# Attention scores with a zero-padded rotated key: every score matmul on 128 rows

## The chip, the cores and the metric

The kernel runs on one core of one Trainium2 chip, as one program. The metric is device time in microseconds (us). TensorE does the matmuls (in the profile PE, and PEld for its weight loads), VectorE is DVE, ScalarE is ACT, GpSimd is POOL, and SyncE (SP) issues most of the transfers.

## The reference, cut to what matters

The model is a trunk of four layers on 256 tokens of width 1024, all in float32. Layer 1 mixes tokens by multi-head latent attention with 8 heads. A query or key of a head has 128 plain values and 64 rotated ones, and the rotated key is the same for all heads:

```
q_rope = apply_rope(q_rope, cos, sin)
k_rope = apply_rope(k_rope[:, :, None, :], cos, sin)
k_rope = jnp.broadcast_to(k_rope, (B, S, MLA_HEADS, MLA_ROPE))
q = jnp.concatenate([q_nope, q_rope], axis=-1)
k = jnp.concatenate([k_nope, k_rope], axis=-1)
...
s = jnp.einsum('bqhd,bkhd->bhqk', qi, k).astype(jnp.float32) * scale
s = jnp.where(kpos[None, :] <= qpos[:, None], s, -jnp.inf)
p = jax.nn.softmax(s, axis=-1).astype(v.dtype)
```

A score is therefore a sum over 128 + 64 products.

## The kernel before, in words

Activations lie with their features on the 128 partitions and the 256 tokens along the free dimension. Projections are done in three matmuls each (`mm3`, L237 to L240): the weights and the activations are split into a high and a low part of type fp32r, and high times high, high times low and low times high are added up. Weights come by DMA in pieces of 1 MB (`raw`), and ScalarE casts the high part (`wh`, L207), VectorE subtracts for the low part (`wl`, L208). A Tile scheduler puts the instructions of every engine into an order at build time, and each engine then works through its own list, waiting on semaphores.

Layer 1 is the function `mla`. The tile `qr` has 8 slices of 256 columns: slices 0 to 3 hold the rotated queries, two heads to a slice (an even head in partitions 0 to 63, an odd one in 64 to 127), slice 4 the rotated key `kr`, which stands in both halves of the partitions alike, slices 5 and 6 the cosines `cs` and sines `sn`, and slice 7 the causal `mask`. `rope` makes a rotated slice in three VectorE steps (L733 reads the cosines, L734 the sines, L735 adds). The plain queries and keys are `qn` and `kn`; the keys are copied out of PSUM by ScalarE, two heads at a time (L765).

The loop behind `es = []` runs over heads. In turn h it issues, in this order, the scores of head h, in turn 1 the values (`vv`, L771, and ScalarE's copies L772), the transposes of head h - 2 (`turn`, L809), and the weighing of head h - 3 (`weigh`, L818 to L820). From head 2 on the transposes follow the scores at once. Between them stand steps of the output projection (`wo`) and of the conditioning vectors (`adaps`, L293, matmuls with 32 output columns).

`scores(h)` makes four matmuls into one PSUM tile `sc`: for the first 128 queries against 128 keys, and for the second 128 against 256 keys, each time a plain one on 128 rows (L788) and a rotated one on 64 rows (L789), which adds to it. They are plain float32, not fp32r; the trace has two records for each of them ("x2"). Behind them VectorE adds the mask (L791), takes the maximum (L792) and scales it (L793), ScalarE takes the exponential (L795), VectorE inverts the sum (L796), and the two share the normalization (L799, L801). Its result `e` is what `turn` transposes; ScalarE copies that to `pts` (L811).

Of the kernel before, what the change touches and what calls it, by code (L numbers as in the profile page):

```python
# [20 lines left out]
P = 128  # L21
# [70 lines left out]
def build(ctx, tc, A, out, stages=None):  # L92
    nc = tc.nc
    pe, act, dve, pool = nc.tensor, nc.scalar, nc.vector, nc.gpsimd
# [8 lines left out]
    def big(name, shape=(P, 2048), dt=F32):  # L103
        return tp.tile(list(shape), dt, tag="big", name=name, bufs=10)
# [4 lines left out]
    def t2(name, shape=(P, 512), dt=F32):  # L109
        return tp.tile(list(shape), dt, tag="t2", name=name, bufs=3)  # L110

    def sm(name, w, dt=F32):
        return tp.tile([P, w], dt, tag="sm", name=name, bufs=6)
# [4 lines left out]
    def misc(name, shape=(P, 512)):  # L118
        return pp.tile(list(shape), F32, tag="misc", name=name, bufs=3)
# [353 lines left out]
    def hilo(name, n):  # L473

        t = [[], []]
        for i in range((n + 7) // 8):
            for e in range(2):
                t[e].append(big(f"{name}{'hl'[e]}{i}", (P, 8, S), F32R))

        def view(e):  # L480
            def at_(c, w=1):
                v = t[e][c // 8]
                return v[:, c % 8, :] if w == 1 else v[:, c % 8 : c % 8 + w, :]

            return at_

        return view(0), view(1)
# [209 lines left out]
    def mla(l):  # L697
# [3 lines left out]
        qr = tables.pop()  # L701
        kr, cs, sn = (qr[:, i, :] for i in (4, 5, 6))
# [64 lines left out]
        def values(b, w=w):  # L767
            for t in range(2):
# [2 lines left out]
                mm3(ps[:], ch[:, 2, t * P : t * P + P], cl[:, 2, t * P : t * P + P], a, bl, True, True)  # L771
                act.copy(vv[:, t, 512 * b : 512 * b + 512], ps[:])  # L772

        yh, yl = hilo("o", 8)
        mask = qr[:, 7, :]
        pool.memset(mask, 0.0)
# [1 line left out]
        spans = ((0, P), (P, S))  # L778

        def scores(h):  # L780
            r0 = 64 * (h % 2)
            s = misc("sc")
            e = t2("e", (P, 384))
            mx = sm("mx", 2)
            nb = sm("nb", 2)
            su = sm("su", 2)
            for t, (o, n) in enumerate(spans):
                pe.matmul(s[:, o : o + n], qn[:, h, t * P : t * P + P], kn[:, h, :n], start=True, stop=False)  # L788
                pe.matmul(s[:, o : o + n], qr[r0 : r0 + 64, h // 2, t * P : t * P + P], kr[r0 : r0 + 64, :n], start=False, stop=True)  # L789
            for t, (o, n) in enumerate(spans):  # L790
                dve.tensor_tensor(e[:, o : o + n], s[:, o : o + n], mask[:, S - n : S], op=ALU.add)  # L791
                dve.tensor_reduce(mx[:, t : t + 1], e[:, o : o + n], axis=AX.X, op=ALU.max)  # L792
            dve.tensor_scalar_mul(nb[:], mx[:], -scale)  # L793
            for t, (o, n) in enumerate(spans):
                act.activation(e[:, o : o + n], e[:, o : o + n], AF.Exp, bias=nb[:, t : t + 1], scale=scale, accum_out=su[:, t : t + 1])  # L795
            dve.reciprocal(su[:], su[:])  # L796
            for t, (o, n) in enumerate(spans):
                if ESACT >> t & 1:
                    act.activation(e[:, o : o + n], e[:, o : o + n], AF.Copy, scale=su[:, t : t + 1])  # L799
                else:  # L800
                    dve.tensor_scalar_mul(e[:, o : o + n], e[:, o : o + n], su[:, t : t + 1])  # L801
            return e
# [22 lines left out]
        for h in range(8 + LAG + OLAG):  # L825
            if h < 8:
                es.append(scores(h))
            for b in range(2):
                if h == VVAT[b]:
                    values(b)  # L830
            if LAG <= h < 8 + LAG:
                turn(h - LAG, es[h - LAG])
            i = h - LAG - OLAG
            if i >= 0:
                weigh(i)
                if i % 2:
                    wo.step(i // 2)
            if h < MLA_ADA:
                ada_run("p")
# [324 lines left out]
    for kind, l in stages:  # L1164
# [3 lines left out]
        if kind == "mix":  # L1168
# [33 lines left out]
            elif l == 1:  # L1202
                modulated(l, 0)
                mla(l)
            else:
                modulated(l, 0)
                hgrn(l)
# [102 lines left out]
```

## Time and profile before

| | |
|---|---|
| time, median of 3 runs | 1388.17 us (1386.49 to 1388.37) |
| the profiled execution: its time, and its span from first to last instruction | 1391.3 us, 1389.6 us |
| PE busy in the span | 1358.8 us (98%) |
| DVE busy | 1091.6 us (79%) |
| ACT busy | 770.8 us (55%) |
| POOL busy | 17.2 us (1%) |
| granted TensorE clock, mean | 0.995 |

Times in the rows of the trace are from the start of the span. A busy share counts overlapping matmuls once, so a PE at 98% can still lose time between its matmuls: how far apart two matmuls start says more than how long each record is.

### The profile page before, as it was taken

How to read it: one execution, taken by the hardware profiler on the slowest of the kernel's cores; microseconds unless marked ns; L12 is line 12 of the kernel's file. 1: busy time of each engine (PE TensorE's matmuls, PEld its weight loads, DVE VectorE, ACT ScalarE, POOL GpSimd, SP SyncE). 2: the span in 40 equal slices, each digit the busy share in tenths (PEclk: the TensorE clock that was granted, in tenths of full speed). 3: DMA queues.
4: the chain of work that ended last, by engine and by line, in shares of the span. 5: the costliest groups of instructions: out<-in, count | busy, mean ns of one | idle time of the engine just before them, and what ended most of it. 6: DMA issues, size and time to landing. Idle time of an engine off the chain costs nothing.

```text
span 1389.6 us, 29284 instructions
## 1 busy us (share of the span) xinstructions
PE 1358.8 (98%) x12372; PEld 1286.1 (93%) x12372; DVE 1091.6 (79%) x1760; ACT 770.8 (55%) x1201; POOL 17.2 (1%) x17
## 2 busy tenths in 40 slices
PE   8999999999999999999989999999999999999997
PEld 6799999999987899999987889999987999999997
DVE  5699698889786698897788879889764964888853
ACT  3764366664465566654655646665456653666633
POOL 0100000000000000000010000000001000000000
PEclk9999999999999999999999999999999999999999
DMA  9869955468775276589475577558737465455531
GB/s 383 330 249 337 379 189 214 178 215 346 324 273 213 98 263 245 211 331 372 173 271 194 235 281 296 194 208 322 254 125 258 178 217 182 151 184 182 183 122 31
DMA packets 49483, 326.23 MB, mean 235 GB/s; under 512 B 5956, under 2 KB 9028, under 8 KB 11974
## 3 DMA queue, kind: packets, MB, share of 16 engines
q1 hardware_dynamic: 47568, 322.72, 61.9%
q8 instruction: 97, 1.59, 0.5%
q10 hardware_dynamic: 1784, 1.65, 0.4%
q14 instruction: 34, 0.28, 0.1%
HBM read 323.29 MB, written 1.05 MB: 233 GB/s over the span
## 4 chain that ended last, share of the span: by engine, by line
PE 92%; DVE 3%; DMA 3%; ACT 2%; issue 1%; DVEq 0%; SPq 0%; ACTq 0%
PE up L239 12%; PE up L238 12%; PE up L240 12%; PE dn L238 4%; PE dn L239 4%; PE dn L240 4%; PE go L238 2%; PE go L239 2%; PE go L240 2%; PE u L239 2%; PE u L238 2%; PE u L240 2%; PE adaps L293 2%; PE v L238 2%; PE v L239 2%; PE v L240 2%
## 5 line engine op out<-in xcount | busy, mean ns | idle before, releaser
L207 ACT CAST wh<-raw 128x1024 fp32r<-128x1024 f32 x426 | 434.9, 1031 | 395.5 <-PE up L239 171.4
L208 DVE TENSOR_TENSOR wl<-raw,wh 128x1024 fp32r<-128x1024 f32 x426 | 511.7, 1206 | 162.9 <-ACT wh L207 160.9
L238 PE MATMUL up<-hh,wh 128*128 128x256 f32 x1408 | 398.4, 284 | 2.6 <-ACT hh L444 2.5
L240 PE MATMUL up<-hh,wl 128*128 128x256 f32 x1408 | 398.3, 283 | 0.0
L239 PE MATMUL up<-hlo,wh 128*128 128x256 f32 x1408 | 398.2, 284 | 0.1
L238 PEld LDWEIGHTS up<-hh,wh 128*128 128x128 f32 x1408 | 270.5, 192 | 5.3 <-ACT hh L444 4.5
L239 PEld LDWEIGHTS up<-hlo,wh 128*128 128x128 f32 x1408 | 270.4, 192 | 0.6 <-DVE hlo L445 0.5
L240 PEld LDWEIGHTS up<-hh,wl 128*128 128x128 f32 x1408 | 270.8, 193 | 0.0
L238 PE MATMUL dn<-gh,wh 128*128 128x256 f32 x528 | 149.9, 284 | 1.5 <-ACT y L1089 1.5
L239 PE MATMUL dn<-gl,wh 128*128 128x256 f32 x528 | 149.4, 283 | 0.0
L240 PE MATMUL dn<-gh,wl 128*128 128x256 f32 x528 | 149.4, 283 | 0.0
L315 DVE CUSTOM_DVE_ANT_0 adaw<-adaw,cbc,prm 128x1024 f32<-128x1024 f32 x104 | 131.3, 1276 | 2.2 <-DMA adaw<-adad 2.2
L1089 ACT ACTIVATE y<-up,cwb 128x256 f32<-128x256 f32 x176 | 98.6, 560 | 10.1 <-DVE y L1091 9.8
L238 PEld LDWEIGHTS dn<-gh,wh 128*128 128x128 f32 x528 | 101.3, 192 | 2.0 <-ACT y L1089 1.7
L239 PEld LDWEIGHTS dn<-gl,wh 128*128 128x128 f32 x528 | 101.3, 192 | 0.0
L240 PEld LDWEIGHTS dn<-gh,wl 128*128 128x128 f32 x528 | 101.3, 192 | 0.0
L1091 DVE SCALAR_TENSOR_TENSOR y<-up,cwb,y 128x254 f32<-128x254 f32 x176 | 84.5, 480 | 4.7
L1090 DVE SCALAR_TENSOR_TENSOR y<-up,cwb,y 128x255 f32<-128x255 f32 x176 | 83.9, 477 | 0.8 <-ACT y L1089 0.8
L238 PE MATMUL u<-hh,wh 128*128 128x256 f32 x256 | 73.9, 289 | 0.0
L238 PE MATMUL go<-yh,wh 128*128 128x256 f32 x256 | 73.3, 287 | 0.0
L240 PE MATMUL u<-hh,wl 128*128 128x256 f32 x256 | 72.4, 283 | 0.0
L239 PE MATMUL u<-hlo,wh 128*128 128x256 f32 x256 | 72.4, 283 | 0.0
(337 smaller groups left out, 2478.8 us busy)
## 6 DMA issues: line engine op xcount, KB each, us to landing
raw<-up SPq DMA_DIRECT2D x88, 1024.0 KB, 4.8
adaw<-adad SPq DMA_DIRECT2D x52, 1024.0 KB, 8.1
adaw<-adap SPq DMA_DIRECT2D x36, 1024.0 KB, 7.5
raw<-dn SPq DMA_DIRECT2D x32, 1024.0 KB, 4.8
raw<-gmu SPq DMA_DIRECT2D x16, 1024.0 KB, 4.8
raw<-gmo SPq DMA_DIRECT2D x16, 1024.0 KB, 4.8
raw<-gmv SPq DMA_DIRECT2D x15, 1024.0 KB, 6.3
raw<-dn SPq DMA_DIRECT2D x16, 768.0 KB, 5.5
```

Of the source, the lines that this page charges most:

```text
L207: act.copy(wh[:, :w], raw[:, o : o + w])
L208: i = dve.tensor_tensor(wl[:, :w], raw[:, o : o + w], wh[:, :w].bitcast(F32), op=ALU.subtract)
L238: pe.matmul(ps, lh, rh, start=start, stop=False)
L239: pe.matmul(ps, lh, rl, start=False, stop=False)
L240: i = pe.matmul(ps, ll, rh, start=False, stop=stop)
L293: pe.matmul(ps[32 * j : 32 * j + 32, :], crep(kc), raw[:, k, j, :], start=kc == 0, stop=kc == KC - 1, tile_position=(0, 32 * j))
L315: dve.tensor_tensor_reduce(raw[:, e, :], raw[:, e, :], cbc[:], 1.0, prm[:, c0 : c0 + 1], ALU.mult, ALU.add, mod[:, l, b : b + 1])
L1089: act.activation(y[:], ps[:, e, :], AF.Identity, bias=b, scale=w[2])
L1090: dve.scalar_tensor_tensor(y[:, 1:], ps[:, e, : S - 1], w[1], y[:, 1:], op0=ALU.mult, op1=ALU.add)
L1091: dve.scalar_tensor_tensor(y[:, 2:], ps[:, e, : S - 2], w[0], y[:, 2:], op0=ALU.mult, op1=ALU.add)
```

## The change

Slice 5 of `qr`, whose cosines are not read after the last rotated query, becomes a second key `kro`. ScalarE copies the lower half of the key (partitions 64 to 127) there; GpSimd then writes zeros into that half of `kr`, and into partitions 0 to 63 of `kro`. So `kr` holds the key for even heads over zeros, and `kro` zeros over the key for odd heads. The rotated matmul now takes all 128 partitions of the query slice, which holds both heads of a pair, and the zeros take the other head's products out of the sum. The scores are the same.

```
+        kro = qr[:, 5, :]
+        act.copy(kro[64:P, :], kr[64:P, :])
+        pool.memset(kr[64:P, :], 0.0)
+        pool.memset(kro[0:64, :], 0.0)
+        krs_ = (kr, kro)
...
         def scores(h):
-            r0 = 64 * (h % 2)
             s = misc("sc")
...
                 pe.matmul(s[:, o : o + n], qn[:, h, t * P : t * P + P], kn[:, h, :n], start=True, stop=False)
-                pe.matmul(s[:, o : o + n], qr[r0 : r0 + 64, h // 2, t * P : t * P + P], kr[r0 : r0 + 64, :n], start=False, stop=True)
+                pe.matmul(s[:, o : o + n], qr[:, h // 2, t * P : t * P + P], krs_[h % 2][:, :n], start=False, stop=True)
```

Every engine keeps its order otherwise; three instructions are added, and lines behind them move down by 5. On ScalarE this is the place just before the first scores, with the semaphores that each waits for; `kn` are the plain keys, `wh` casts of later weights. Before:

```order
L207 CAST wh_1024_4912<-raw_4822 128x1024 [waits PE_49,Activation_49]
L207 CAST wh_0_5137<-raw_4906 128x1024 [waits DMAHW2_49,DVE_49,PE_49]
L765 COPY kn<-kn 128x512 [waits PE_49] x3
L207 CAST wh_1024_5141<-raw_4906 128x1024 [waits DVE_49,PE_49]
L765 COPY kn<-kn 128x512 [waits PE_49]
L772 COPY vv<-vv 128x512 [waits DMAHW1_49,PE_49,Pool_49]
```

And with the change:

```order
L207 CAST wh_0_5140<-raw_4906 128x1024 [waits DMAHW2_49,DVE_49,PE_49]
L765 COPY kn<-kn 128x512 [waits PE_49]
L776 COPY qr<-qr 64x256 [waits DVE_49]
L765 COPY kn<-kn 128x512 [waits PE_49] x2
L207 CAST wh_1024_5144<-raw_4906 128x1024 [waits PE_49,Activation_49]
L765 COPY kn<-kn 128x512 [waits PE_49]
L772 COPY vv<-vv 128x512 [waits DMAHW1_49,PE_49,Pool_49]
```

The copy of the key stands between the first and the second copy of plain keys. The semaphore value that it waits for on VectorE belongs to the last reading of the cosines (L733 for the fourth pair of heads).

On TensorE these are the scores of the first two heads, between the plain keys and the values. Before:

```order
L240 MATMUL kn<-chl,wl_0_4825 128x256
L788 MATMUL sc<-kn,qn 128x128
L789 MATMUL sc<-qr 128x128
L788 MATMUL sc<-kn,qn 128x256
L789 MATMUL sc<-qr 128x256
L788 MATMUL sc<-kn,qn 128x128
L789 MATMUL sc<-qr 128x128
L788 MATMUL sc<-kn,qn 128x256
L789 MATMUL sc<-qr 128x256
L238 MATMUL vv<-wh_1024_4828,chl 128x512 [waits DVE_49]
```

And with the change:

```order
L793 MATMUL sc<-kn,qn 128x128
L794 MATMUL sc<-qr 128x128 [waits Pool_49]
L793 MATMUL sc<-kn,qn 128x256
L794 MATMUL sc<-qr 128x256
L793 MATMUL sc<-kn,qn 128x128
L794 MATMUL sc<-qr 128x128 [waits Activation_49]
L793 MATMUL sc<-kn,qn 128x256
L794 MATMUL sc<-qr 128x256
L238 MATMUL vv<-wh_1024_4828,chl 128x512 [waits DVE_49]
```

The matmuls stand as before (the sizes are those of the output); the first rotated one now waits for GpSimd's second memset, and the first one of an odd head for ScalarE's copy. GpSimd's two memsets stand behind those of the mask, which run much earlier; the first waits for that last reading of the cosines, the second for ScalarE's copy.

## Rows read from the trace of the kernel before

**Rows 1.** The page, part 4: shares of the chain that ended last, by engine.

```profile
PE 92%; DVE 3%; DMA 3%; ACT 2%; issue 1%; DVEq 0%; SPq 0%; ACTq 0%
```

**Rows 2.** Windows: busy us of PE, PEld, DVE, ACT, POOL; clock; DMA.

```profile
404.00:450.00 46.00, 46.00 (x310) 35.21 (x309) 31.69 (x86) 25.44 (x65) 0.00 (x0) 1.00 0.59 229
```

**Rows 3.** Timeline of PE, heads 0 and 1: start, us, engine, line, what.

```profile
407.84 0.39 PE L788 MATMUL sc<-kn,qn 128*128 128x128 f32 x2
408.16 0.48 PE L789 MATMUL sc<-qr 64*128 64x128 f32 x2
408.57 0.70 PE L788 MATMUL sc<-kn,qn 128*128 128x256 f32 x2
409.20 0.70 PE L789 MATMUL sc<-qr 64*128 64x256 f32 x2
409.83 0.49 PE L788 MATMUL sc<-kn,qn 128*128 128x128 f32 x2
410.25 0.48 PE L789 MATMUL sc<-qr 64*128 64x128 f32 x2
410.66 0.70 PE L788 MATMUL sc<-kn,qn 128*128 128x256 f32 x2
411.29 0.70 PE L789 MATMUL sc<-qr 64*128 64x256 f32 x2
411.92 0.50 PE L238 MATMUL vv<-wh,chl 128*128 128x512 f32 x1
412.25 0.39 PE L239 MATMUL vv<-wl,chl 128*128 128x512 f32 x1
412.48 0.39 PE L240 MATMUL vv<-wh,chl 128*128 128x512 f32 x1
```

**Rows 4.** Timeline of PE: transposes and weighing, behind scores and behind `wo`.

```profile
416.76 0.55 PE L809 MATMUL pt<-ident,e 128*128 128x128 f32 x3
...
419.13 0.55 PE L809 MATMUL pt<-ident,e 128*128 128x128 f32 x3
419.51 0.39 PE L818 MATMUL po<-pts,vv 128*128 128x128 f32 x2
419.74 0.39 PE L819 MATMUL po<-pts,vv 128*128 128x128 f32 x2
419.96 0.39 PE L820 MATMUL po<-pts,vv 128*128 128x128 f32 x2
...
455.19 0.49 PE L809 MATMUL pt<-ident,e 128*128 128x128 f32 x3
455.51 0.39 PE L818 MATMUL po<-pts,vv 128*128 128x128 f32 x2
```

**Rows 5.** Timeline of PE: two float32 matmuls of 512 columns in layer 0.

```profile
63.03 1.88 PE L598 MATMUL rsum<-ws,ones 128*128 128x512 f32 x4
```

**Rows 6.** Line L818: its weight loads, ns min/median/max, first and last start.

```profile
L818 PEld LDWEIGHTS po<-pts,vv x16: 186/190/192, 419.4 to 456.4; 128*128 128x128 f32 x16
```

**Rows 7.** Timeline of ACT around the first scores.

```profile
405.99 1.91 ACT L765 COPY kn<-kn 128x512 f32<-128x512 f32 x3
...
412.96 0.59 ACT L772 COPY vv<-vv 128x512 f32<-128x512 f32 x1 [3.51 <-issue]
...
415.27 0.41 ACT L799 ACTIVATE e<-e,su 128x128 f32<-128x128 f32 x1
...
417.26 0.40 ACT L799 ACTIVATE e<-e,su 128x128 f32<-128x128 f32 x1 [0.24 <-DVE su L796]
```

**Rows 8.** Timeline of DVE around the first scores.

```profile
405.16 0.42 DVE L733 TENSOR_TENSOR ra<-q,qr 128x256 f32<-128x256 f32 x1 [0.35 <-PE q L240]
...
412.02 0.29 DVE L791 TENSOR_TENSOR e<-sc,qr 128x128 f32<-128x128 f32 x1 [0.74 <-PE sc L789]
```

**Rows 9.** Timeline of POOL: two of its memsets.

```profile
177.71 0.32 POOL L776 MEMSET qr<- 128x256 f32 x1 [114.68 <-PE adaps L293]
...
699.74 1.06 POOL L980 MEMSET hs<- 128x1024 f32 x1 [521.21 <-ACT hp L910]
```

## The prediction, made before the changed kernel was run

> **What bounds the kernel now.** First the chain that ended last: PE has 92% of it [rows 1], so a step pays only if it takes time from PE, or from what PE waits for. Then the stretch of the change: in the 46 us around the eight heads' scores PE is busy 46.00, at a granted clock of 1.00, which is the upper level of 2.4 GHz [rows 2]; no wait of PE is listed there. VectorE is busy 31.69 of the 46 and ScalarE 25.44, so both have room. Whatever PE saves here moves everything behind it, since those two do their casts and softmax steps when PE gives them buffers or scores. Third, inside PE, the timeline of the first two heads: not how long a record is but how far apart two matmuls start [rows 3]. Each matmul of 64 rows stands between matmuls of 128 rows, and there the distances are too long for the columns, as follows.
>
> **What a float32 matmul costs when the row count does not change.** 128 columns: the weighing matmuls start at 419.51, 419.74 and 419.96 [rows 4], 0.22 to 0.23 apart; I take 0.22. 256 columns on 128 rows between others of 128 rows are not in the trace, so I work them out: two matmuls of 512 columns, four records, take 1.88 [rows 5]; with a record of 0.59 (its tail, which the next one overlaps, included) that leaves (1.88 - 0.59) / 3 = 0.43 from record to record. A record of the 128-column case stands 0.11 from the next, a quarter, so the cost goes by columns and a record of 256 takes 0.215, two of them 0.43. The slope agrees: L789 itself takes 0.22 more for 128 more columns (0.63 against 0.41, below).
>
> **What it costs now** [rows 3], start to next start in head 0: L788 with 128 columns 0.32 (407.84 to 408.16), L789 with 128 columns 0.41, L788 with 256 columns 0.63, L789 with 256 columns 0.63. Against 0.22, 0.22, 0.43, 0.43 that is 0.10 + 0.19 + 0.20 + 0.20 = 0.69 too much. I read it as two halves of about 0.1 at each change of the row count: the matmul before must be out, and the first load after is not hidden. So the next instruction pays too: L788 of head 1 takes 0.42 instead of 0.32, 0.10 more; the first value matmul takes 0.33 against 0.23 of the second, 0.10; and three transposes behind scores take 0.38 (419.13 to 419.51), behind `wo` 0.32 (455.19 to 455.51) [rows 4], 0.06.
>
> Ahead of this reading stands a statement of the Trainium skill, "TensorEngine Tiling (Array Packing)", section Key Properties: a change of the tiling mode, and not just of the tile, drains the engine. It gives no figure, and the rows above give one.
>
> **The change, part by part.**
>
> Removed: the change of row count at all 32 rotated matmuls. Inside the heads 8 x 0.69 = 5.52. Behind them, head 0 into head 1 0.10, head 1 into the values 0.10, and six heads (2 to 7) into transposes 6 x 0.06 = 0.36. Sum 6.08 us off PE. Three heads that follow the 32-column `adaps` matmuls keep their entry cost, which I have not counted as gain.
>
> Added on PE: nothing. The rotated matmul has the same columns and the same count; the doubled rows cost nothing if a full matmul costs by its columns, which the weighing rows, on 128 rows, carry already.
>
> Added on ScalarE: one copy of 64x256, between the first and second copy of keys. It waits for the last reading of the cosines, done at 405.16 + 0.42 = 405.58 [rows 8], before the first key copy starts at 405.99 [rows 7], so it does not hold ScalarE. No copy of that shape is in the rows; ScalarE's 128-column pass takes 0.40 to 0.41 and a 512-column copy 0.59 [rows 7], so I take 0.4 and bound it by 0 and 0.6. The three key copies take 1.91 because each waits for PE's next keys; at 3 x 0.59 = 1.77 without a wait, and with neighbours overlapping, most of the copy falls in those waits, at most 0.6 stays. The first user of a later key copy is head 2, behind the values. Cost nothing; without that cover 0.4.
>
> Added on GpSimd: two memsets of 64x256, on an engine with no other work within 100 us. The first can run from 405.58, the second once the copy is done, about 406.6 + 0.4 = 407.0. Price: the memset of 128x256 took 0.32, that of 128x1024 1.06 [rows 9]; I take 0.32, the nearer shape, and 0 and 1.06 as ends. The zeros then stand at 407.3 (upper end 408.1). The first rotated matmul, which now waits for them, comes at 407.84 + 0.22 = 408.06. So the wait is covered by 0.7, and costs 0 to 0.1; if it came late, every matmul behind it on PE would be late by as much.
>
> Late next: PE reaches `turn(0)` 0.69 + 0.79 + 0.10 + 0.68 = 2.26 earlier (heads 0 and 1 with their exits, and head 2), at 416.76 - 2.26 = 414.50. The softmax of head 0 was done at 415.27 + 0.41 = 415.68 [rows 7], 1.08 ahead of PE. Does it move too? Its exponential stands on ScalarE behind the first value copy at 412.96, which had waited for the value matmuls on PE; those come 0.69 + 0.79 + 0.10 = 1.58 earlier. The maximum it needs is ready in time: VectorE had idled 0.74 for PE [rows 8]. So `e` of head 0 is ready at 414.10, 0.40 ahead of PE. Head 1: ready at 417.66 [rows 7], 416.08 when it moves by 1.58; PE at `turn(1)` 419.13 - 2.26 - 0.06 - 0.69 = 416.12. That is no margin, so I give 0 to 0.3 back here. From head 3 on whole steps of the output projection lie between scores and transposes. So the sum is 6.08, with bounds of 5.5 (0.1 at the zeros, 0.3 at head 1, the rest in rounding) and 6.4.
>
> **The sum.** The profiled execution took 1391.3 (span 1389.6 and 1.7 around it), and would take 1385.2. It lies 3.1 above the median of the runs, 1388.17; from the median the forecast is 1388.17 - 6.08 = **1382.1 us**, 0.44% less. About 0.2%, or 2.8 us, is what a measurement can tell here from no change.
>
> **The rivals.**
>
> *Part of it is given back.* PE gets ahead of the softmax of heads 0 to 2, or ahead of casts or transfers later on, and stands still instead. For it: the margin at head 1 is nil, and VectorE is 79% busy over the span. Against it: both engines' idle time in this stretch ends on PE. If half of the first three heads' saving goes (about 1.1) and another 1 later, the gain is about 4: 1384.2.
>
> *The row count is not what costs.* The extra 0.2 could come from adding to columns just written, which stays. For it: each rotated matmul adds to the plain one before it. Against it: L820 adds to L819's columns on 128 rows, 0.22 on [rows 4], and the extra stands as well ahead of L788, which starts a new sum. Time 1388.2.
>
> *Slower: the loads come out of cover.* With 128 rows everywhere a weight load might have to wait for the running matmul, where now it goes to other rows. A load takes 0.19 [rows 6] and a head has 8 passes: 8 x 0.19 = 1.52 on the bare 1.30 (0.22 + 0.22 + 0.43 + 0.43), 2.82 a head against some 2.06 now with its exit, 8 x 0.76 = 6.1 more: 1394.3. It decides once more than 6.08 / 64 = 0.095 of each load is uncovered. Against it: the weighing matmuls load new weights for each of two passes, 2 x 0.19 = 0.38, and start 0.22 apart, so most of a load is under the pass before.
>
> That rule stands in the Trainium skill, "TensorE: Matmul & The Clock Gate", section Part 3: Packing small matmuls: weight loads overlap matmuls in flight only when their row group differs. The rows of the weighing differ from it; by the rule the time would be the rival's, 1394.3, by the rows 1382.1.
>
> **How the numbers follow.** The full gain (5.3 to 6.6) 0.74: the distances are read, not modelled, and PE is the chain there. Part of it (2.8 to 5.3) 0.13; row count not the cause, or all absorbed, 0.09; slower 0.04. The first two are faster by over 0.2%: 0.87, same 0.09, slower 0.04. The likeliest case has 1381 to 1383.5, with the runs' own spread of 1.9 (1386.49 to 1388.37). The range takes in most of the partial case and leaves out the last two: 1380.0 to 1386.5.
>
> **What would show it.** Right: in heads 0 to 7 the four score matmuls start 0.22, 0.22, 0.43 and 0.43 apart (0.32 for the first behind `adaps`), some 1.3 a head; first value matmul 0.23; three transposes 0.32; first rotated matmul with no wait for GpSimd; memsets done before 408. Wrong: distances unchanged with 128 rows in the record; idle PE before `turn(0)` or `turn(1)` until ScalarE or VectorE; a wait for POOL before 408.06; or the gain there at 450 and gone by the end of the layer's FFN, which would mean that something other than PE sets the pace behind it.

## The result, and the profile after

| | before | after |
|---|---|---|
| time, median of 4 runs each | 1388.27 us (1386.49 to 1389.01) | 1378.35 us (1377.02 to 1381.63) |
| ratio, with its 95% interval | | 0.9933 (0.992 to 0.9945) |
| the profiled execution: time, span | 1391.3, 1389.6 us | 1377.02, 1375.2 us |
| PE busy | 1358.8 us | 1348.0 us |
| granted clock, mean | 0.995 | 0.998 |

The change saves 9.9 us of median. The forecast was 6.1 less and a range that ended at 1380.0: right in sign, too small by 3.8. The scores did what was predicted. Something else won about as much, 300 us later, in another layer.

**The scores.** The timeline of PE of the changed kernel, for the first two heads, the transposes behind head 2 and the last transposes (start, us, engine, line, what):

```profile
407.45 0.39 PE L793 MATMUL sc<-kn,qn 128*128 128x128 f32 x2
407.68 0.39 PE L794 MATMUL sc<-qr 128*128 128x128 f32 x2
407.90 0.60 PE L793 MATMUL sc<-kn,qn 128*128 128x256 f32 x2
408.33 0.59 PE L794 MATMUL sc<-qr 128*128 128x256 f32 x2
408.77 0.38 PE L793 MATMUL sc<-kn,qn 128*128 128x128 f32 x2
...
410.31 0.39 PE L239 MATMUL vv<-wl,chl 128*128 128x512 f32 x1
...
414.15 0.49 PE L814 MATMUL pt<-ident,e 128*128 128x128 f32 x3
414.48 0.39 PE L793 MATMUL sc<-kn,qn 128*128 128x128 f32 x2
...
448.87 0.49 PE L814 MATMUL pt<-ident,e 128*128 128x128 f32 x3
449.20 0.39 PE L823 MATMUL po<-pts,vv 128*128 128x128 f32 x2
```

Against [rows 3], the distances are 0.23, 0.22, 0.43 and 0.44 where they were 0.32, 0.41, 0.63 and 0.63: head 0 takes 1.32 instead of 1.99. The transposes take 0.33. No row has an idle time behind it, so PE waited neither for the zeros nor for the softmax. From the first score to the last transposes it takes 448.87 - 407.45 = 41.42, before 455.19 - 407.84 = 47.35 [rows 3, 4]: 5.93 us less.

The zeros come early enough. POOL's timeline, and ACT's for the copy of the key:

```profile
405.32 0.31 POOL L778 MEMSET qr<- 64x256 f32 x1 [227.20 <-DVE ra L733]
406.73 0.31 POOL L777 MEMSET qr<- 64x256 f32 x1 [1.10 <-ACT qr L776]
```

```profile
406.21 0.40 ACT L776 COPY qr<-qr 64x256 f32<-64x256 f32 x1
```

They stand at 407.04, and the first rotated matmul starts at 407.68.

**What else moved.** The two profiled executions lie 14.4 us of span apart, more than the medians' 9.9: that of before was 3.1 slower than its median, that of after 1.3 faster. Following the same instructions through both: 0.4 is there at the first score already, 5.9 comes from the scores, 1.5 lies between them and VectorE's copy at L979 in layer 2 (699.71, now 691.89, 7.8 earlier), 6.3 within 35 us behind that copy, and 0.3 behind that. The place is the function `hgrn`. At its first tree level VectorE copies one half of a tile (L979, `dve.tensor_copy(Sf, Ps)`) and GpSimd writes zeros into the other (L980, `pool.memset(Ss, 0.0)`); both are released by the same ScalarE instruction (L910, which writes `hp`). Before, VectorE's timeline shows there a copy of 3.36 us, and later a wait for a transfer:

```profile
699.71 3.36 DVE L979 COPY hs<-hp 128x1024 f32<-128x1024 f32 x1 [1.14 <-ACT hp L910]
...
718.65 1.28 DVE L315 CUSTOM_DVE_ANT_0 adaw<-adaw,cbc,prm 128x1024 f32<-128x1024 f32 x1 [2.22 <-DMA adaw<-adad]
...
723.34 0.68 DVE L953 TENSOR_TENSOR hsg<-hq,hk 128x512 f32<-128x512 f32 x1
```

POOL's two memsets behind the one in [rows 9], before:

```profile
700.72 1.80 POOL L916 MEMSET at<- 128x2048 f32 x1
702.47 1.07 POOL L917 MEMSET haa<- 128x512 f32 x1
```

After, VectorE's copy and then POOL's three memsets:

```profile
691.89 0.70 DVE L984 COPY hs<-hp 128x1024 f32<-128x1024 f32 x1 [1.14 <-ACT hp L915]
```

```profile
691.97 1.62 POOL L985 MEMSET hs<- 128x1024 f32 x1 [284.93 <-ACT hp L915]
693.53 1.80 POOL L921 MEMSET at<- 128x2048 f32 x1
695.28 0.52 POOL L922 MEMSET haa<- 128x512 f32 x1
```

Read the two together. One engine works and the other stands, as if they shared a door. Before, the rows fit a copy that makes no headway until the second memset ends at 702.52 and then takes the 0.55 that are left to 703.07; the third memset takes 1.07 instead of 0.52, longer by just that much. After, the copy has its 0.70 and the first memset is 1.62 instead of 1.06 long, again about the time of the copy. What goes with it is when GpSimd starts: 0.03 us behind the copy's recorded start, and GpSimd has the door; 0.08 behind, and VectorE has it. The Trainium skill, "SBUF — State Buffer", section Who interferes with whom, has the rule: VectorE in a mode that uses two ports (a copy can enter it) and GpSimd share a pair of ports, whoever issues first holds it for the whole instruction, and the other is blocked, not slowed. The 1.62 and the 3.36 agree with it; but here the copy waited for two memsets (1.06 and 1.80), not for one, and no trace names the mode that the copy ran in.

Those 2.66 us reach PE by a way that the chain of the kernel before shows (start, us, what):

```profile
708.81 0.60 DVE hsg L953
709.41 0.42 DVE adaw L315
709.83 0.71 issue
710.64 7.99 DMA adaw<-adad
```

VectorE is late with `adaw`, so its buffer comes free late, so the next transfer into it starts late; VectorE waits for that, and is late with the last `hsg`, for which PE stands. PE before and after, at the first `psum` of this level, the matmul that it stands before, and at the second, which comes behind matmuls of `hi`:

```profile
720.17 0.39 PE L239 MATMUL hi<-wl,hh 128*128 128x512 f32 x1
724.08 1.94 PE L937 MATMUL psum<-hsg,ones 128*32 128x512 f32 x8 [3.52 <-DVE hsg L953]
...
731.21 0.64 PE L937 MATMUL psum<-qk,ones 128*32 128x256 f32 x8
```

```profile
712.35 0.39 PE L239 MATMUL hi<-wl,hh 128*128 128x512 f32 x1
712.67 1.07 PE L942 MATMUL psum<-hsg,ones 128*32 128x512 f32 x8
...
717.07 0.64 PE L942 MATMUL psum<-qk,ones 128*32 128x256 f32 x8
```

Up to the first `psum` it is 3.91 us before and 0.32 after. Then 7.13 against 4.40, because TensorE's clock had fallen, from 2.4 to 1.2 GHz, behind the idle stretch. The windows show it, before and, for the same work 11.4 us earlier, after (busy us of PE, PEld, DVE, ACT, POOL; clock; DMA):

```profile
723.00:730.00 7.00, 5.92 (x18) 3.38 (x19) 5.04 (x6) 0.00 (x0) 0.00 (x0) 0.51 1.00 398
```

```profile
711.60:718.60 7.00, 7.00 (x40) 4.30 (x39) 6.04 (x8) 2.10 (x2) 0.00 (x0) 1.00 0.89 350
```

Together 3.59 + 2.73 = 6.3 us in this pair of executions.

**Why it turned.** GpSimd's memset of `hs` carries a long list of waits, most of them for work long done. The built order of GpSimd with its semaphores, before:

```
L980 MEMSET hs 128x1024 [waits DMAHW1_49,DMAHW2_49,DMAHW0_49,DMAHW4_49,DVE_49,DMAHW7_49,PE_49,Activation_49]
```

and after:

```
L985 MEMSET hs 128x1024 [waits DMAHW1_49,DMAHW0_49,DMAHW2_49,DVE_49,DMAHW4_49,PE_49,DMAHW7_49,Activation_49,Pool_49]
```

The ninth semaphore is GpSimd's own and stands for the new zeros in the upper partitions of `qr`. Why the scheduler asks for it is not shown: by the addresses in the built program `hs` does not lie where `qr` lay, but in the block beside it, which `kn` had. The wait has long been met, but it stands behind ScalarE's, and that changes where ScalarE's wait is done. In the built program only the last wait of such a list stands on the memset itself; the others stand, one or two each, on four semaphore instructions ahead of it, which only wait. The last of these four, before and after (least, median and greatest time in ns, here of one, and its start in us):

```profile
L980 POOLq EVENT_SEMAPHORE  x1: 43/43/43, 698.7 to 698.7; - x1
```

```profile
L985 POOLq EVENT_SEMAPHORE  x1: 972/972/972, 690.9 to 690.9; - x1
```

Before, it passes in 0.04 and the memset itself waits for ScalarE. After, it waits 0.97 for ScalarE, and only then comes the memset, which starts 0.08 instead of 0.03 behind the copy. So theory A: 5 to 6 us from the scores, some 5 from one more wait in layer 2. Theory B: the scores made all of the gain, and layer 2 differs by chance or because it is reached earlier.

### The profile page after: what moved, and what is told of

It reads as the page before. It is cut to its first block, busy times and chain, and to the rows that moved or that the text cites. A ratio compares the mean times of both kernels' runs of the same rounds, so it can differ in the third digit from the quotient of the medians.

```text
span 1375.2 us, 29290 instructions
## 1 busy us (share of the span) xinstructions
PE 1348.0 (98%) x12372; PEld 1283.2 (93%) x12372; DVE 1088.5 (79%) x1760; ACT 770.8 (56%) x1202; POOL 17.6 (1%) x19
## 4 chain that ended last, share of the span: by engine, by line
PE 92%; DMA 2%; DVE 2%; ACT 2%; issue 1%; DVEq 0%; SPq 0%; ACTq 0%
PE up L238 12%; PE up L239 12%; PE up L240 12%; PE dn L238 5%; PE dn L239 4%; PE dn L240 4%; PE go L238 2%; PE go L239 2%; PE go L240 2%; PE u L239 2%; PE u L238 2%; PE u L240 2%; PE adaps L293 2%; PE v L238 2%; PE v L239 2%; PE v L240 2%
```

## The experiments

Each is named by its edit. In the first four the kernel before took 1388.41 us (12 runs), in the last three 1388.53 (20 runs); the ratios are against these.

**64 rows again, all else kept.** The changed kernel, whose rotated matmuls read 64 rows as before:

```
+            r0 = 64 * (h % 2)
-                pe.matmul(s[:, o : o + n], qr[:, h // 2, t * P : t * P + P], krs_[h % 2][:, :n], start=False, stop=True)
+                pe.matmul(s[:, o : o + n], qr[r0 : r0 + 64, h // 2, t * P : t * P + P], krs_[h % 2][r0 : r0 + 64, :n], start=False, stop=True)
```

> The copy of the key and both memsets stay as in the changed kernel, but the rotated matmuls read their 64 rows again, from kr for even and kro for odd heads. Theory A: the change of row count costs 0.69 us in a head and 0.06 to 0.1 behind it, and the surplus over that comes from layer 2, where GpSimd's memset of hs now waits for one more semaphore and VectorE's copy of hp gets in first. Then the four score matmuls stand 0.32 or 0.42, 0.41, 0.63, 0.63 apart again, the copy takes 0.7 instead of 3.36, and the time is 3 to 4.5 below before: about 1384.5. Theory B: the surplus is chance of single executions and has nothing to do with the added instructions: time as before, 1388, and the copy at 3.36.

Measured: 1383.41 us (1382.53 to 1384.41), ratio 0.9964 (0.9952 to 0.9977), 5.0 less. The score distances are the old ones, and layer 2 is as in the changed kernel (the copy 0.70, the memset of `hs` 1.62, no wait at `psum`). PE's timeline, head 0:

```profile
407.18 0.39 PE L794 MATMUL sc<-kn,qn 128*128 128x128 f32 x2
407.50 0.48 PE L795 MATMUL sc<-qr 64*128 64x128 f32 x2
407.92 0.70 PE L794 MATMUL sc<-kn,qn 128*128 128x256 f32 x2
408.54 0.70 PE L795 MATMUL sc<-qr 64*128 64x256 f32 x2
```

So half of the gain has nothing to do with the rows of the matmuls; the other half goes with them, since the rows are all that tells this kernel from the changed one.

**The zeros by ScalarE.** The changed kernel without GpSimd's new writes:

```
-        pool.memset(kr[64:P, :], 0.0)
-        pool.memset(kro[0:64, :], 0.0)
+        act.activation(kr[64:P, :], kr[64:P, :], AF.Copy, scale=0.0)
+        act.activation(kro[0:64, :], kr[0:64, :], AF.Copy, scale=0.0)
```

> Scores on 128 rows as in the changed kernel, but the zeros are written by ScalarE (a copy with scale 0), so that GpSimd has no new work and its memset of hs in layer 2 waits for the same semaphores as before. Theory A: 1.30 us a head as in the changed kernel, but VectorE's copy of hp takes 3.36 again and PE waits some 3.5 us for hsg: 5.5 to 6.5 below before, about 1382. Theory B: as the changed kernel, about 1378.4.

Measured: 1383.11 us (1381.14 to 1384.7), ratio 0.996 (0.9947 to 0.9972), 5.3 less. The scores keep their gain but for short waits in the first two heads: from the first score to the second value matmul it takes 410.04 - 406.82 = 3.22, where the changed kernel has 2.86 and the kernel before 4.41. The copy is back at 3.36, and PE stands 3.29 before `psum`:

```profile
692.77 3.36 DVE L984 COPY hs<-hp 128x1024 f32<-128x1024 f32 x1 [1.14 <-ACT hp L915]
```

```profile
406.82 0.39 PE L793 MATMUL sc<-kn,qn 128*128 128x128 f32 x2
...
410.04 0.40 PE L239 MATMUL vv<-wl,chl 128*128 128x512 f32 x1
...
716.91 1.90 PE L942 MATMUL psum<-hsg,ones 128*32 128x512 f32 x8 [3.29 <-DVE hsg L958]
```

This is the half of the scores, and 5.0 + 5.3 = 10.3 is the 9.9 of the change within the intervals.

**The memset of `hs` on VectorE**, in the kernel before:

```
-                    pool.memset(Ss, 0.0)
+                    dve.memset(Ss, 0.0)
```

> The kernel before, with the one memset of hs in layer 2 (L980) done by VectorE instead of GpSimd; scores untouched. Theory A: VectorE's copy takes about 0.7 and its memset some 0.7 to 1.1 more, PE's wait for hsg of 3.5 us goes to under 1, and with it the stretch at half clock behind it: 3 to 6 below before, about 1384. Theory B: no change, 1388.

Measured: 1382.92 us (1382.53 to 1385.07), ratio 0.9965 (0.9953 to 0.9977), 5.5 less with no change to the scores. VectorE's timeline:

```profile
697.72 0.70 DVE L979 COPY hs<-hp 128x1024 f32<-128x1024 f32 x1 [1.13 <-ACT hp L910]
698.58 0.91 DVE L980 MEMSET hs<- 128x1024 f32 x1 [0.16 <-issue]
```

VectorE does both in 1.77 us, where beside GpSimd the copy alone took 3.36. GpSimd's other two memsets, no longer queued behind that of `hs`, ran from 662.78 on.

**The score matmuls regrouped.** The kernel before, with both plain matmuls of a head first and then both of 64 rows:

```
-                pe.matmul(s[:, o : o + n], qn[:, h, t * P : t * P + P], kn[:, h, :n], start=True, stop=False)
-                pe.matmul(s[:, o : o + n], qr[r0 : r0 + 64, h // 2, t * P : t * P + P], kr[r0 : r0 + 64, :n], start=False, stop=True)
+                pe.matmul(s[:, o : o + n], qn[:, h, t * P : t * P + P], kn[:, h, :n], start=t == 0, stop=False)
+            for t, (o, n) in enumerate(spans):
+                pe.matmul(s[:, o : o + n], qr[r0 : r0 + 64, h // 2, t * P : t * P + P], kr[r0 : r0 + 64, :n], start=False, stop=t == 1)
```

> The kernel before with the four score matmuls of a head in another order: both plain ones, then both rotated ones on 64 rows. Two changes of row count a head instead of four. If the change of row count costs 0.2 us (theory A), 0.4 a head goes: 3.1 below before, about 1385. If a matmul of 64 rows is slow by itself, nothing: 1388; L789 would still take 0.41 and 0.63 to its next start. Layer 2 as before in both.

Measured: 1385.43 us (1383.59 to 1387.25), ratio 0.9977 (0.9966 to 0.9987), 3.0 less. PE's timeline, heads 0 and 1 (records of the two sizes are run together, so a row has four):

```profile
407.75 0.82 PE L788 MATMUL sc<-kn,qn 128*128 128x128 f32 x4
408.50 0.92 PE L790 MATMUL sc<-qr 64*128 64x128 f32 x4
409.35 0.92 PE L788 MATMUL sc<-kn,qn 128*128 128x128 f32 x4
410.20 0.92 PE L790 MATMUL sc<-qr 64*128 64x128 f32 x4
411.05 0.50 PE L238 MATMUL vv<-wh,chl 128*128 128x512 f32 x1
```

A head takes 1.60 behind the keys and 1.70 behind another head, 0.39 less than before with two changes of the row count fewer: 0.2 us a change. The columns and the rows are those of before, so 64 rows are not slow by themselves. The regrouping also puts a matmul between a plain one and the one that adds to its columns, so this run alone does not rule out that the adding costs; the changed kernel does, where each rotated matmul adds to columns just written and the distances are 0.22 and 0.43. The copy took 3.36 here too.

**An idle write that brings the ninth wait.** The kernel before, with a memset whose zeros nobody reads:

```
-        pool.memset(mask, 0.0)
+        pool.memset(mask, 0.0); pool.memset(qr[64:P, 5, :], 0.0)
```

> The kernel before with one idle instruction more: GpSimd writes zeros into partitions 64 to 127 of slice 5 of qr behind the mask, which nobody reads afterwards; the scores stay on 64 rows. In the built order the only differences are this memset, one wait for GpSimd in a late VectorE step, and that layer 2's GpSimd memset of hs now waits for nine semaphores instead of eight, GpSimd's own being the ninth. Theory A (the ninth wait lets VectorE's copy of 128x1024 start before GpSimd's memset in layer 2): copy about 0.70, memset some 80 ns behind it and about 1.62 long, no wait of PE over 0.5 at psum, time 1383 (1382 to 1384.5). Rival B (the shorter scores bring layer 2 into another state, the wait does nothing): copy 3.36, time 1388.4.

Measured: 1383.53 us (1382.18 to 1387.55), ratio 0.997 (0.9957 to 0.9984), 5.0 less. Its rows on VectorE, GpSimd and PE are those of the changed kernel:

```profile
697.95 0.70 DVE L979 COPY hs<-hp 128x1024 f32<-128x1024 f32 x1 [1.14 <-ACT hp L910]
```

```profile
698.03 1.62 POOL L980 MEMSET hs<- 128x1024 f32 x1 [292.25 <-ACT hp L910]
```

```profile
718.73 1.06 PE L937 MATMUL psum<-hsg,ones 128*32 128x512 f32 x8
```

**Its twin, without the ninth wait.** The same memset in the other half of the partitions, `qr[0:64, 5, :]`; here the memset of `hs` keeps eight semaphores.

> The twin of the run with the idle write in partitions 64 to 127: the same memset, of the same size and at the same place of GpSimd's order, but in partitions 0 to 63. Here the memset of hs keeps its eight waits. Theory A (the ninth wait decides): copy 3.36, memset of hs 1.06, PE waits about 3 at psum, time 1388.4 (1387 to 1389.5), 5 more than its twin. Rival B: as its twin at 1388.4. Rival C (any GpSimd write more in this buffer does it): as its twin at 1383.

Measured: 1388.39 us (1386.42 to 1391.06), ratio 1.0002 (0.9991 to 1.0013).

```profile
697.40 3.37 DVE L979 COPY hs<-hp 128x1024 f32<-128x1024 f32 x1 [1.14 <-ACT hp L910]
```

```profile
697.42 1.06 POOL L980 MEMSET hs<- 128x1024 f32 x1 [292.23 <-ACT hp L910]
```

```profile
721.74 1.94 PE L937 MATMUL psum<-hsg,ones 128*32 128x512 f32 x8 [3.49 <-DVE hsg L953]
```

The twins have the same instructions in the same order on every engine, and on all engines but GpSimd the same waits. They are 4.9 us apart by one more wait that is met long before, and by where it puts the wait for ScalarE (the idle memset itself also waits for the mask's, 290 us earlier). Theory B falls: both reach the copy in layer 2 within 0.6 us of each other, 697.95 and 697.40.

**Both cures at once.** The changed kernel, with the memset of `hs` on VectorE:

> The changed kernel with layer 2's memset of hs on VectorE instead of GpSimd. Theory A (in the changed kernel the two engines no longer collide there, so nothing is left to win): within 1.5 of the changed kernel's 1378.4, the copy stays at 0.70 and VectorE has 0.91 more to do. Rival (moving the memset is worth its own 5.5, as on the kernel before, on top of the change): 1372.9.

Measured: 1378.61 us (1376.4 to 1382.21), ratio 0.9933 (0.9916 to 0.995): no further gain. The move was worth 5.5 in the kernel before and nothing here, so both take away the same collision. It is the version to keep all the same: it takes the two engines apart, where the changed kernel only happens to start them 0.05 us more apart. That half of the change's gain is luck: nothing in the change aims at it.

## Why the prediction was wrong in size

*What bounds the kernel now* and *What a float32 matmul costs when the row count does not change*: right. PE sets the pace in that stretch, the score matmuls cost 0.22 and 0.43, and full matmuls of 128 rows with new weights each start without a gap.

*Removed*: right (its "32 rotated matmuls" are 16 of two records each, but the sum goes by heads), 6.08 predicted and 5.93 measured from the first score to the last transposes; from the first score to the second value matmul 1.55 (410.31 - 407.45 = 2.86, against 4.41) where the two heads with their exits gave 1.58. The regrouped kernel agrees with the reading behind it, 0.2 us for each change of the row count; how that splits into a late start and an open load is not shown.

*Added on PE, Added on ScalarE*: right; the copy took 0.40, and only GpSimd waited for it (1.10), not PE. *Late next*: `turn(0)` at 414.15 and `turn(1)` at 415.79 run without a wait, so nothing was given back.

*Added on GpSimd*: this step failed. It priced the two memsets (0.32, measured 0.31) and asked whether the first reader of the zeros would wait. It did not ask whose list of waits grows by these writes. That of GpSimd's memset of `hs` does, 285 us later: by its ninth semaphore it starts 0.05 us later, and VectorE has the first turn; the twins show that this wait decides. The term is -5.0 (the idle write), not 0 to 0.1. [rows 9] held the memset of that collision, 699.74 and 1.06 long, and I used it as a mere price of a memset; VectorE's copy beside it, at 3.36 for what takes 0.70, was in the same trace. *The sum* was therefore 6.08 where 5.93 and about 5 belong.

*The rivals*: "part of it is given back" and "the row count is not what costs" are refuted by the distances in the changed kernel. That both engines' idle time in this stretch ends on PE was read too widely: from 404 to 460 VectorE waits 5.3 us for ScalarE's exponentials and 5.2 for its casts. It cost nothing here. "The loads come out of cover" would show as 8 x 0.19 more a head; head 0 takes 1.32, so that rule of the Trainium skill ("TensorE: Matmul & The Clock Gate", Part 3: Packing small matmuls) does not hold for these float32 matmuls. That a collision between other engines might end was not among the rivals.

What stays open: why the scheduler gives the memset of `hs` the ninth wait, and why 0.03 and 0.08 fall on either side, which no run varied finely. Half-clock stretches also come and go between executions: that at 470 us in the profile of before is missing after, and stands in that of the run with 64 rows (granted clock 0.91 from 460 to 480). The changed kernel with the memset on VectorE has one too (0.91), the twins, with the old scores, none (1.00). It lies in the 1.5 us between the scores and layer 2, so nothing shows these to be a gain of the change.

## What to carry to other kernels

Where a small matmul of fewer rows stands between full ones, count the changes of the row count before the columns: here 0.2 us each, and zeros in the missing rows cost nothing. When a change writes into a buffer from another engine, look in the built order for every later instruction whose list of waits grows, see which wait then stands on the instruction itself and which ahead of it, and look in the trace at what starts beside it. And when the same operation takes 0.70 in one place and 3.36 in another, ask what runs on GpSimd at that moment.

## What was not expected of the hardware

VectorE's plain copy of 128x1024 takes 0.70 us alone and 3.36 or 3.37 when GpSimd's memsets win; in all seven runs and both kernels it is one of the two. GpSimd won when its memset was recorded 0.02 to 0.03 us behind the copy, VectorE when it was 0.08. The 0.02 to 0.03 go with a memset that waited for ScalarE itself, the later start with a semaphore instruction that did so for 0.97 us ahead of it. A copy that had lost was let in behind the second of three memsets that ran without a gap, not behind the first. An idle stretch of 3.5 us on PE was followed by half the clock: 1.94 us for the eight `psum` matmuls instead of 1.07.
